# Delta rule in a hybrid layer: the correction of the chunk inverse in 16-bit pairs, its updates in place on the changed halves, the decay bias on ScalarE

## The chip, the core and the metric

The kernel runs on one core of one Trainium2 chip. The metric is the device time of one execution in microseconds; smaller is better. The engines are named as the profile names them: PE (TensorE, matmuls; PEld is its weight loads), DVE (VectorE), ACT (ScalarE), POOL (GpSimd) and SP (SyncE, which issues the DMAs).

## The reference

One layer of a hybrid encoder over 2048 prompt tokens and 64 tokens of a running stream, with 1024 features. RMSNorm and one input projection feed two groups: a gated delta rule with 4 heads of 128 and a multi-scale pooling group. Both go through one output projection, then a SwiGLU feed-forward and a final norm. Everything is float32. The change lies in the delta rule, which the reference computes by chunks in WY form (cut to what matters):

```python
G = jnp.cumsum(g, axis=-1)
gamma = jnp.exp(jnp.where(lower_incl, G[..., :, None] - G[..., None, :], -jnp.inf))
kb = k * beta[..., None]
Lm = jnp.where(lower_strict, jnp.einsum('bhncd,bhnsd->bhncs', kb, k) * gamma, 0.0)
T = lax.linalg.triangular_solve(eye + Lm, jnp.broadcast_to(eye, Lm.shape),
                                left_side=True, lower=True)
u = jnp.einsum('bhncs,bhnsv->bhncv', T, v * beta[..., None])
w = jnp.einsum('bhncs,bhnsk->bhnck', T, kb * jnp.exp(G)[..., None])
...
def step(S, xs):
    u_c, w_c, qk_c, qd_c, kt_c, dl_c = xs
    v_new = u_c - jnp.einsum('bhck,bhkv->bhcv', w_c, S)
    o_c = jnp.einsum('bhck,bhkv->bhcv', qd_c, S) + jnp.einsum('bhcs,bhsv->bhcv', qk_c, v_new)
    S = S * dl_c[..., None, None] + jnp.einsum('bhck,bhcv->bhkv', kt_c, v_new)
    return S, o_c
```

For every chunk of every head a unit triangular matrix is inverted; this inverse, and the decay matrix gamma, are what the change touches.

## The kernel before

The prompt is cut into four blocks of 512 tokens; the 64 tokens of the running stream ride with block 0. For each block the kernel projects (tiles `pp`, matmuls of 512 or 288 columns in a rounded 32-bit form, each product three matmuls of high and low parts), makes the decays (`rows`), and runs per head four chunks of 128 tokens. Between these run the pooling group and the output projection of the block before (tiles `pz`). After the last block follows the feed-forward, from 996 us on; it holds no work of the delta rule.

A head of a block is worked on by two kinds of chains. A *front* (`Front.all`, line 921) takes two chunks at once and needs no state: it makes the decay matrix, the products of k with k and q, and the inverse. There are 32 fronts of the prompt and one of the running stream. A *head* (`Head.prompt`, line 1071) then carries the state S through the chunks in order, with five small 32-bit matmuls per chunk (tiles `pk`, `po`).

In a front, every tile holds both chunks side by side, 128 partitions x 256 elements. These are its steps:

- **Decay.** `gb` gets the cumulated decay of each column by a matmul with `selp` (`rowmm`). ACT takes its exponential into EG. Then into the same bank go the mask `negm` (16-bit) and the negated decay of each row: two matmuls per front with `seln` as moving operand (`negmm`, line 908). ACT takes the exponential of all of it into `Gam`.
- **The matrix.** `gr` holds the products; U (tile `Gst`) is the strictly triangular matrix to be inverted (with 1 on the diagonal implied).
- **Levels.** The inverse T and its transpose V are built by doubling, seven levels for chunks of 128. In level l blocks of size 2^l are joined to blocks of twice that size. GpSimd masks U (`Um`), PE multiplies (`py`, 2 matmuls; ACT copies the result to `Yt`; `pt`, 4 matmuls), and DVE subtracts: `new` = TV - pt. These operands are 16-bit. TV holds T and V of both chunks, 512 elements, and is written anew in each level, in turns `TV0` and `TV1`, and in the last level in 32 bits, `TV32`.
- **Correction.** T from 16-bit arithmetic is corrected by two steps in 32 bits: F = I - T - U'T (GpSimd, `pf`, DVE), then T1 = V + F'V (`px0`, DVE) and X = V + F'T1 (`px1`, DVE). Each of the three products is one 32-bit matmul per chunk, so six in a front.

A bank of PSUM is set aside for each of three fronts that run at a time (`NLEV` = 3, banks b0 to b2); the tiles `gb`, `gr`, `py`, `pt`, `pf`, `px` of a front follow one another in its bank.

What sets the order: the kernel first records all operations, then a planner (`Machine.issue`) puts them on the engines' queues by its own reckoning of durations, dependences and ranks, and writes every engine's queue in that order. Therefore nearly all instructions have the line 278, and the views below go by tiles. On PE the planner prefers work of the fronts and heads and fills the gaps with dense matmuls. It places an instruction of PE 0.25 us behind the moment at which it reckons its operand ready (`MARGIN`). Each engine takes its queue strictly in that order. A 32-bit matmul stands as one instruction in the order and as two records in the trace.

Of the kernel before, what the change touches and what calls it, by code (L numbers as in the profile page):

```python
# [27 lines left out]
NH = 4  # L28
# [325 lines left out]
def hybrid_kernel(ctx, tc, a, o):  # L354
# [496 lines left out]
    nc.vector.tensor_copy(id16, ident)  # L851
    idbf = cp1.tile([P, P], BF16, tag="idbf", name="idbf")
# [7 lines left out]
    nc.vector.memset(Sp, 0.0)  # L860

# [6 lines left out]
    class Front:  # L868
# [39 lines left out]
        def negmm(self, ps):  # L908

            G = self.B.Ghl  # L910
            if self.h is None:
                for h in range(NH):
                    mm(ps[:, h * DEC : (h + 1) * DEC], G[:, SO : SO + P], seln[:, h, :].to_broadcast([P, DEC]),
                       start=False, stop=False)
            else:
                for c in range(2):
                    at = self.off + c * C
                    mm(ps[:, c * C : (c + 1) * C], G[:, at : at + C], seln[:, self.h, :].to_broadcast([P, C]),
                       start=False, stop=c == 1, skip_group_check=True)

        def all(self):
# [14 lines left out]
            for c in range(2):  # L936
# [17 lines left out]
            dd = gb if self.h is not None else self.ps(f"dd_{tag}")  # L954
            mm(dd[:, : 2 * C], idbf, bc(negm2 if self.h is None else negm, 2, C), start=dd is not gb, stop=False,
               skip_group_check=dd is gb)
            self.negmm(dd)
            if dd is not gb:
                self.rowmm(dd, False)
            Gam = self.QKG = gt([P, 2, C], F32, "Gam", NOUT)  # L960
            act(Gam, two(dd), AF.Exp)
# [17 lines left out]
            for l in range(nlev):  # L979
                Um = lev(F16, "Um", l, bufs=2)  # L980
                nc.gpsimd.tensor_tensor(out=Um, in0=U, in1=bc(lmask[:, l], 2, C), op=ALU.mult)
                new = TV32 if l == nlev - 1 else lev(F16, f"TV{l % 2}", l, [P, 2, 2, C])
# [3 lines left out]
                if l == 0:  # L986
                    idb = bc(id16, 2, C)
                    tt(new[:, 0], idb, two(py), ALU.subtract)
                    nc.gpsimd.tensor_tensor(out=new[:, 1], in0=idb, in1=Um, op=ALU.subtract)
                else:  # L990
# [796 lines left out]
```

## Time and profile before

| | us |
|---|---|
| Median of 3 runs | 2384.84 |
| Lowest and highest | 2381.84, 2387.46 |
| The profiled execution | 2383.12 |
| Its span, first to last instruction | 2380.5 |
| Mean granted clock of PE | 0.997 |

How to read the views used below. The page gives each engine's busy time. The view by stretches gives the same for parts of the span, in microseconds from its start. Rows of groups name engine, operation, tile written <- tiles read, shape and count, then busy time, mean duration in ns, and idle time before them with what ended it. Rows of a tile give minimum, median and maximum duration in ns. The waits of an engine give who waited <- for whom, the total, how often, and the longest. The timeline gives start, length of a run of equal instructions from first start to last end, and their count; consecutive matmuls overlap, since a matmul starts before the one ahead has drained. The chain of the work that ended last gives pieces with their start and length.

### The profile page before, as it was taken

The page shows a single profiled execution, that of the slowest core. Times are in us where ns is not written, and L with a number is a line of the kernel's source. Part 1 is how long each engine was busy: PE and PEld are TensorE (multiplying, and loading weights), DVE is VectorE, ACT ScalarE, POOL GpSimd, SP SyncE. Part 2 cuts the span into 40 slices and gives each one's busy share as a digit, 9 for nine tenths or more (in the row PEclk, how much of TensorE's full clock was granted, in tenths as well). Part 3 has the DMA queues.
Part 4 walks back from the last instruction along what each step waited for, and adds up shares of the span by engine and source line. Part 5 has one row for each costly group of instructions (what it writes and reads, how often), then busy time and mean ns, then how long its engine had stood idle before and what let it go on. Part 6 is the DMA issues. An engine that isn't in the chain of part 4 may idle for free.

```text
span 2380.5 us, 41651 instructions
## 1 busy us (share of the span) xinstructions
PE 2344.3 (98%) x14823; PEld 2184.7 (92%) x14823; DVE 1674.3 (70%) x2943; ACT 1215.7 (51%) x2738; POOL 967.2 (41%) x1130
## 2 busy tenths in 40 slices
PE   9999999999999999999999999999999999999998
PEld 8999798777887778899999999999999999999998
DVE  7999875785577686787776883767566657646466
ACT  6666654564456565574454654553334554425334
POOL 1656452554346662264332536353233464202211
PEclk9999999999999999999999999999999999999999
DMA  7643566445555565998876678887855697565763
GB/s 267 224 165 134 189 228 217 146 165 190 176 182 172 162 195 166 311 373 324 312 282 240 257 270 271 295 287 248 283 189 175 201 348 247 193 227 193 260 209 114
DMA packets 228384, 540.57 MB, mean 227 GB/s; under 512 B 28240, under 2 KB 86608, under 8 KB 228176
## 3 DMA queue, kind: packets, MB, share of 16 engines
q1 hardware_dynamic: 228176, 537.92, 66.2%
q8 instruction: 116, 1.90, 0.3%
q14 instruction: 92, 0.75, 0.1%
HBM read 389.41 MB, written 148.41 MB: 226 GB/s over the span
## 4 chain that ended last, share of the span: by engine, by line
PE 81%; DVE 9%; ACT 3%; DMA 3%; issue 2%; SPq 1%; POOL 1%; DVEq 0%; POOLq 0%; ACTq 0%
PE px L278 19%; PE pp L278 14%; PE pz L278 11%; PE py L278 9%; PE d L278 8%; PE dx L278 5%; PE dy L278 3%; PE pk_p L278 2%; PE pt_p L278 1%; PE dz L278 1%; PE gr_p L278 1%; PE px_p L278 1%; DVE Yqk L278 1%; PE py_p L278 1%; ACT E L278 1%
## 5 line engine op out<-in xcount | busy, mean ns | idle before, releaser
L278 PE MATMUL pp<-h,wsp 128*128 128x512 f32 (+1 forms) x2480 | 562.1, 366 | 2.0 <-DVE h L278 1.7
L278 PEld LDWEIGHTS pp<-h,wsp 128*128 128x128 f32 x2480 | 402.3, 190 | 49.8 <-DVE h L278 2.6
L278 POOL TENSOR_TENSOR Um_p<-Gst_p,lmask 128x256 f16<-128x256 f32 x224 | 178.2, 809 | 109.6 <-PE py_p L278 80.9
L278 PE MATMUL pz<-op,wsp 128*128 128x512 f32 (+1 forms) x960 | 216.8, 366 | 3.4 <-ACT op L278 2.9
L278 PE MATMUL d<-h3l,wsd 128*128 128x352 f32 x1248 | 201.3, 322 | 0.2 <-DVE h3l L278 0.2
L278 PEld LDWEIGHTS d<-h3l,wsd 128*128 128x128 f32 x1248 | 199.1, 188 | 1.2 <-DVE h3l L278 0.7
L278 PEld LDWEIGHTS pz<-op,wsp 128*128 128x128 f32 x960 | 155.9, 190 | 23.2 <-ACT op L278 3.4
L278 DVE TENSOR_TENSOR TV_p<-TV_p,pt_p 128x512 f16<-128x512 f16 (+1 forms) x192 | 128.5, 681 | 48.7 <-PE pt_p L278 43.4
L278 PE MATMUL px<-hA,ws 128*128 128x352 f32 x792 | 141.2, 322 | 0.6 <-DMA ws<-g 0.6
L278 PE MATMUL pz<-hB,ws 128*128 128x352 f32 x792 | 139.6, 322 | 0.6 <-DMA ws<-g 0.6
L278 PE MATMUL px<-hBT,ws 128*128 128x352 f32 x792 | 137.8, 322 | 2.1 <-DVE u L278 2.1
L278 PE MATMUL px<-hBT,wsS 128*128 128x352 f32 x792 | 137.7, 322 | 2.0 <-ACT g L278 1.9
L278 PE MATMUL py<-hB,wsS 128*128 128x352 f32 x792 | 139.2, 322 | 0.1
L278 PE MATMUL px<-hA,wsS 128*128 128x352 f32 x792 | 137.4, 322 | 0.9 <-ACT g L278 0.9
L278 PE MATMUL py<-hA,wsS 128*128 128x352 f32 x792 | 137.1, 322 | 0.0
L278 ACT ACTIVATE hr<-g 128x352 f32<-128x352 f32 x132 | 65.6, 497 | 133.4 <-DVE g L278 133.4
L278 PEld LDWEIGHTS px<-hBT,wsS 128*128 128x128 f32 x792 | 128.2, 188 | 2.8 <-ACT g L278 2.8
L278 PEld LDWEIGHTS px<-hBT,ws 128*128 128x128 f32 x792 | 128.0, 188 | 2.9 <-DVE u L278 2.7
L278 PEld LDWEIGHTS px<-hA,ws 128*128 128x128 f32 x792 | 128.9, 188 | 1.0 <-DMA ws<-g 0.9
L278 PEld LDWEIGHTS pz<-hB,ws 128*128 128x128 f32 x792 | 128.6, 188 | 0.8 <-ACT hB L278 0.8
L278 PEld LDWEIGHTS px<-hA,wsS 128*128 128x128 f32 x792 | 128.3, 188 | 1.2 <-ACT g L278 1.1
L278 PEld LDWEIGHTS py<-hB,wsS 128*128 128x128 f32 x792 | 128.6, 188 | 0.4 <-ACT u L278 0.4
(686 smaller groups left out, 5354.5 us busy)
## 6 DMA issues: line engine op xcount, KB each, us to landing
wsS<-gS SPq DMA_DIRECT2D x176, 512.0 KB, 4.7
ws<-g SPq DMA_DIRECT2D x132, 512.0 KB, 4.6
wsp<-wnd SPq DMA_DIRECT2D x126, 512.0 KB, 3.3
gS<-wsS SPq DMA_DIRECT2D x88, 512.0 KB, 5.6
g<-ws SPq DMA_DIRECT2D x66, 512.0 KB, 5.5
wnd<-wsp SPq DMA_DIRECT2D x42, 512.0 KB, 4.5
xd<-x2d SPq DMA_DIRECT2D x96, 176.0 KB, 4.0
wrd<-in_wd_dram SPq DMA_DIRECT2D x48, 256.0 KB, 4.7
```

The costliest lines, as they stand in the source:

```text
L278: getattr(getattr(self.nc, op.eng), name)(*args, **kw)
```

## The change

- **Correction.** T and V stay 16-bit in the last level too, and `TV32` is gone. U is split into a high and a low 16-bit half, scaled by 256 (`Uhl`, made by ACT and DVE behind level 2). `pf` is then four 16-bit matmuls. F is made on DVE in 32 bits from a 16-bit I - T (GpSimd) and `pf`, and split into halves `Fhl` (ACT, DVE). The first `px` takes the high half alone, two 16-bit matmuls; ACT scales it to 16 bits (`FV`, listed as Ytg). The second `px` stays in the same bank and adds three 16-bit matmuls per chunk: low half of F times V, T against a scaled identity `idfs` (which gives 256 V), high half of F times FV. ACT writes X from it. Both additions on DVE go.
- **Updates in place.** In level l only half of the columns of T and the other half of those of V change. DVE now subtracts on these alone, in one tile TV, through the view `fresh`: runs of 2^l elements with gaps of the same length, 256 elements in place of 512.
- **Decay.** The fronts of the prompt lose the two `seln` matmuls. ACT takes the exponential of each chunk with the negated decay as its bias per partition (`NG`, made once per block in `rows`), so Gam is two instructions of 128 elements. The running stream keeps the old way.
- EG moves from the first part of `TV32` to the tile tag `F`.

```diff
+    idfs = cp1.tile([P, P], F16, tag="idfs", name="idfs")
+    ts(idfs, ident, FS, None, ALU.mult)
...
+    def fresh(t, s):
+
+        (row, n), _ = t.ap
+        return bass.AP(t.tensor, t.offset, [[row, n], [2 * C + s, 2], [2 * s, 2 * C // (2 * s)], [1, s]])
...
-            TV32 = lev(F32, "TV32", "", [P, 2, 2, C])
...
-            EG = TV32[:, 0]
+            EG = lev(F32, "F", "e")
...
-            act(Gam, two(dd), AF.Exp)
+                mm(gb[:, : 2 * C], idbf, bc(negm, 2, C), start=False, stop=True, skip_group_check=True)
+                for c in range(2):
+                    act(Gam[:, c], two(gb)[:, c], AF.Exp, bias=self.B.NG[:, self.c0 + c, self.h : self.h + 1])
...
-                    tt(new, TV, pt.rearrange("p (t c n) -> p t c n", t=2, n=C), ALU.subtract)
-                TV = new
+                    new = fresh(TV.rearrange("p t c n -> p (t c n)"), 1 << l)
+                    tt(new, new, fresh(pt, 1 << l), ALU.subtract)
+                if l == 2:
+                    Uhl = lev(F16, "Uhl", "", [P, 2, 2, C])
+                    act(Uhl[:, 0], U, AF.Copy, scale=FS)
+                    stt(Uhl[:, 1], U, FS, Uhl[:, 0], ALU.mult, ALU.subtract)
                 yield LAT_TV
-            T, V = TV32[:, 0], TV32[:, 1]
-            F = lev(F32, "F")
-            nc.gpsimd.tensor_tensor(out=F, in0=bc(ident, 2, C), in1=T, op=ALU.subtract)
+            T, V = TV[:, 0], TV[:, 1]
+            F0 = lev(F16, "Um", "f", bufs=2)
+            nc.gpsimd.tensor_tensor(out=F0, in0=bc(id16, 2, C), in1=T, op=ALU.subtract)
             pf = self.ps(f"pf_{tag}")
             for c in range(2):
-                mm(pf[:, c * C : (c + 1) * C], U[:, c], T[:, c], start=True, stop=True)
-            tt(F, F, two(pf), ALU.subtract)
+                for i in range(2):
+                    mm(pf[:, c * C : (c + 1) * C], Uhl[:, i, c], T[:, c], start=i == 0, stop=i == 1)
+            F = lev(F32, "F")
+            stt(F, F0, FS, two(pf), ALU.mult, ALU.subtract)
+            Fhl = lev(F16, "Fhl", "", [P, 2, 2, C])
+            nc.scalar.copy(Fhl[:, 0], F)
+            tt(Fhl[:, 1], F, Fhl[:, 0], ALU.subtract)
             yield LAT_F
-            px = self.ps(f"px0_{tag}")
+            px = self.ps(f"px_{tag}")
             for c in range(2):
-                mm(px[:, c * C : (c + 1) * C], F[:, c], V[:, c], start=True, stop=True)
-            tt(T, V, two(px), ALU.add)
+                mm(px[:, c * C : (c + 1) * C], Fhl[:, 0, c], V[:, c], start=c == 0, stop=True, skip_group_check=c > 0)
+            FV = lev(F16, "Yt", "g")
+            act(FV, two(px), AF.Copy, scale=1.0 / FS)
             yield LAT_D
             yield self.before(NX, "used")
             X = self.X = gt([P, 2, C], F32, "X", NX)
-            px = self.ps(f"px1_{tag}")
             for c in range(2):
-                mm(px[:, c * C : (c + 1) * C], F[:, c], T[:, c], start=True, stop=True)
-            tt(X, V, two(px), ALU.add)
+                for i, (lhsT, rhs) in enumerate(((Fhl[:, 1, c], V[:, c]), (T[:, c], idfs), (Fhl[:, 0, c], FV[:, c]))):
+                    mm(px[:, c * C : (c + 1) * C], lhsT, rhs, start=False, stop=i == 2, skip_group_check=True)
+            act(X, two(px), AF.Copy, scale=1.0 / FS)
...
+        NG = B.NG = gp.tile([P, 4, NH], F32, tag="NG", name=f"NG{j}", bufs=2)
+        act(NG[:, :nch], pcs[:, :, :NH], AF.Copy, scale=-1.0)
...
+FS = 256.0
```

How the order changes, at three places. First PE, in the correction of the second front of head 1 in block 1; `pz` are dense matmuls of an output projection. Before:

```order
L278 MATMUL pf_p_1_1_1254<-TV_p_1_1_1141,Gst_p_1_1_1146 128x128 x2
L278 MATMUL pz_5_288_1170<-op_0_165,wsp_36_1070 128x288 x10
L278 MATMUL pz_5_288_1170<-op_0_164,wsp_36_1068 128x288
L278 MATMUL px_p_1_1_1258<-TV_p_1_1_1141,F_p_1_1_1253 128x128 x2
L278 MATMUL pz_5_288_1170<-op_0_164,wsp_36_1068 128x288 x11
L278 MATMUL px_p_1_1_1266<-TV_p_1_1_1141,F_p_1_1_1253 128x128 x2
```

The changed kernel at the same front, from the first `px` on:

```order
L278 LDWEIGHTS Fhl_p_1_1_1235
L278 MATMUL px_p_1_1_1238<-TV_p_1_1_1155,Fhl_p_1_1_1235 128x128
L278 LDWEIGHTS Fhl_p_1_1_1235
L278 MATMUL px_p_1_1_1238<-TV_p_1_1_1155,Fhl_p_1_1_1235 128x128
L278 MATMUL pz_6_0_1166<-op_0_167,wsp_37_1080 128x288 x9
L278 MATMUL pz_6_0_1166<-op_0_166,wsp_37_1078 128x288
L278 LDWEIGHTS Fhl_p_1_1_1235
L278 MATMUL px_p_1_1_1238<-TV_p_1_1_1155,Fhl_p_1_1_1235 128x128
L278 LDWEIGHTS TV_p_1_1_1155
L278 MATMUL px_p_1_1_1238<-idfs,TV_p_1_1_1155 128x128
L278 LDWEIGHTS Fhl_p_1_1_1235
L278 MATMUL px_p_1_1_1238<-Ytg_p_1_1_1239,Fhl_p_1_1_1235 128x128
```

Each product still stands between dense matmuls; the last one is six matmuls (three of them shown) where two stood, every one with a weight load of its own. Second PE, at the decay of the second front of head 2 in block 1, before:

```order
L278 MATMUL gb_p_2_1_1314<-Ghl_822,selp 128x256
L278 MATMUL rpn_20_1279<-lon_20_1281,onesr 128x512
L278 MATMUL pp_12_0_1276<-h_1_774,wsp_42_1222 128x512 x3
L278 MATMUL pp_13_0_1292<-h_1_773,wsp_43_1245 128x512 x3
L278 MATMUL gr_p_2_0_1323<-Yqk_2_1218 128x256
L278 LDWEIGHTS idbf
L278 MATMUL gb_p_2_1_1314<-negm,idbf 128x256
L278 MATMUL gr_p_2_0_1323<-Yqk_2_1218 128x256
L278 MATMUL gb_p_2_1_1314<-seln,Ghl_822 128x128 x2
```

and in the changed kernel:

```order
L278 MATMUL gb_p_2_1_1291<-Ghl_804,selp 128x256
L278 MATMUL pp_12_0_1253<-h_1_743,wsp_42_1198 128x512 x5
L278 LDWEIGHTS idbf
L278 MATMUL gb_p_2_0_1285<-negm,idbf 128x256
L278 LDWEIGHTS idbf
L278 MATMUL gb_p_2_1_1291<-negm,idbf 128x256
L278 MATMUL po_p_2__1455<-Qd_p_2_0_1288,Sp 128x128
```

The two `seln` matmuls are gone, and nothing of PE stands between the mask and ACT's exponential. Third DVE, at the end of the levels of the front of the first place, where `wsp` are splits of weights and `xc` evictions of an output projection. Before:

```order
L278 TENSOR_TENSOR TV_p_1_1_1141<-TV_p_1_1_1228,pt_p_1_1_1248 128x512
L278 TENSOR_TENSOR xc_0_1157<-pz_5_0_1158,xc_0_1157 128x288
L278 TENSOR_TENSOR F_p_1_1_1253<-F_p_1_1_1253,pf_p_1_1_1254 128x256
L278 TENSOR_TENSOR TV_p_1_1_1141<-TV_p_1_1_1141,px_p_1_1_1258 128x256
L278 TENSOR_TENSOR wsp_38_1126<-wrp_38_1125,wsp_38_1126 128x512
L278 TENSOR_TENSOR xc_288_1169<-pz_5_288_1170,xc_288_1169 128x288
L278 TENSOR_TENSOR X_p_1_1_1265<-TV_p_1_1_1141,px_p_1_1_1266 128x256
```

and in the changed kernel:

```order
L278 TENSOR_TENSOR TV_p_1_1_1155<-TV_p_1_1_1155,pt_p_1_1_1228 128x2x2x64
L278 TENSOR_TENSOR xc_0_1135<-pz_5_0_1136,xc_0_1135 128x288
L278 SCALAR_TENSOR_TENSOR F_p_1_1_1234<-Umf_p_1_1_1232,pf_p_1_1_1233 128x256
L278 TENSOR_TENSOR wsp_38_1106<-wrp_38_1105,wsp_38_1106 128x512
L278 TENSOR_TENSOR Fhl_p_1_1_1235<-F_p_1_1_1234,Fhl_p_1_1_1235 128x256
```

The update is half as long, and both additions of `px` have left DVE's queue; the low half of F has come.

More of the change, by code (lines that the diff above doesn't have):

```diff
@@ L910, in negmm @@
             G = self.B.Ghl
[L911 to L919, printed above, removed]
+            for h in range(NH):
+                mm(ps[:, h * DEC : (h + 1) * DEC], G[:, SO : SO + P], seln[:, h, :].to_broadcast([P, DEC]),
+                   start=False, stop=False)
         def all(self):
@@ L953, in all @@
             tt(Qd, self.Yqk[:, 0, self.off : self.off + 2 * C].rearrange("p (c n) -> p c n", n=C), EG, ALU.mult)
[L954 to L958, printed above, removed]
-                self.rowmm(dd, False)
-            Gam = self.QKG = gt([P, 2, C], F32, "Gam", NOUT)
-            act(Gam, two(dd), AF.Exp)
+            Gam = self.QKG = gt([P, 2, C], F32, "Gam", NOUT)
+            if self.h is None:
+                dd = self.ps(f"dd_{tag}")
+                mm(dd[:, : 2 * C], idbf, bc(negm2, 2, C), start=True, stop=False)
+                self.negmm(dd)
+                self.rowmm(dd, False)
+                act(Gam, two(dd), AF.Exp)
+            else:
+                mm(gb[:, : 2 * C], idbf, bc(negm, 2, C), start=False, stop=True, skip_group_check=True)
+                for c in range(2):
+                    act(Gam[:, c], two(gb)[:, c], AF.Exp, bias=self.B.NG[:, self.c0 + c, self.h : self.h + 1])
             U = lev(F32, "Gst")
```

9 lines of the change are left out of this document (5 added, 4 removed).

## The prediction

> **What bounds the kernel now.** I read the page first, then the busy time by stage, then TensorE's (PE's) waits, then the timeline of PE where the changed step runs. The page:
>
> ```profile
> span 2380.5 us, 41651 instructions
> ## 1 busy us (share of the span) xinstructions
> PE 2344.3 (98%) x14823; PEld 2184.7 (92%) x14823; DVE 1674.3 (70%) x2943; ACT 1215.7 (51%) x2738; POOL 967.2 (41%) x1130
> ```
>
> PE is busy 98% of the span. That share alone does not prove it (ends of matmuls are modelled), so I cut the span into the stage in which the fronts run, 60 to 950 us, and the feed-forward stage behind it.
>
> ```profile
> core 0: us, PE busy (x) PEld busy (x) DVE busy (x) ACT busy (x) POOL busy (x), PEclk, DMA share, GB/s
> ...
> 60.00:240.00 180.00, 177.97 (x1466) 165.96 (x1466) 169.81 (x346) 115.67 (x298) 109.72 (x158) 1.00 0.52 176
> 240.00:400.00 160.00, 157.09 (x1053) 138.23 (x1053) 110.38 (x201) 85.48 (x199) 59.20 (x78) 1.00 0.65 217
> 400.00:600.00 200.00, 199.65 (x1229) 159.05 (x1228) 142.55 (x254) 107.38 (x279) 100.39 (x140) 1.00 0.49 166
> 600.00:800.00 200.00, 196.54 (x1156) 158.28 (x1155) 135.11 (x236) 112.66 (x288) 100.41 (x141) 0.99 0.52 170
> 800.00:950.00 150.00, 145.76 (x877) 118.12 (x876) 117.38 (x203) 78.81 (x191) 77.64 (x97) 0.99 0.60 182
> ...
> 1000.00:2380.00 1380.00, 1361.66 (x8476) 1352.95 (x8474) 917.82 (x1529) 646.66 (x1326) 504.56 (x480) 1.00 0.73 253
> ```
>
> In the five pieces of the front stage PE is busy 177.97 + 157.09 + 199.65 + 196.54 + 145.76 = 877.0 of 890 us, at a granted clock of 0.99 to 1.00: 13 us idle in all. DVE is busy 675 us there (76%), ACT 500 (56%), and only in the first piece does another engine come near, DVE with 169.81 of 180 (94%). So what a microsecond of PE work is worth in this stage is nearly a microsecond. And PE hardly waits for the fronts' operands:
>
> ```profile
> PE pk_p L278 <- DVE Sp L278: 1.7, 1, 1.7
> PE pt_p L278 <- ACT Yt_p L278: 1.4, 2, 0.9
> ...
> PE ptv_p L278 <- DVE X_p L278: 0.7, 1, 0.7
> ...
> PE py_p L278 <- DVE TV_p L278: 0.7, 2, 0.5
> ...
> PE px_p L278 <- DVE TV_p L278: 0.4, 1, 0.4
> ```
>
> These five waits come to 4.9 us for 33 fronts. The order puts dense matmuls between the dependent ones of a front, and they hide its chain. Two things follow: shortening the chain on DVE or ACT can win at most a few microseconds, and taking matmul time off PE wins nearly all of it.
>
> **The price of a matmul.** Busy times of small groups hold the drain of each, so I price by starts, from one start to the next.
>
> ```profile
> L278 PE MATMUL pf_p<-TV_p,Gst_p x128: 270/275/328, 90.3 to 941.6; 128*128 128x128 f32 x128
> ...
> L278 PE MATMUL px_p<-TV_p,F_p x256: 270/275/377, 92.8 to 946.2; 128*128 128x128 f32 x128
> ```
>
> ```profile
> 386.03 15.43 PE pp L278 x68
> ```
>
> ```profile
> 401.30 0.60 PE L278 MATMUL ptk_p<-consts,Yqk 128*128 128x128 f32 x4
> ```
>
> ```profile
> 422.27 0.40 PE L278 MATMUL py_p<-TV_p,Um_p 128*128 128x128 f16 x4
> 422.47 1.87 PE L278 MATMUL pp<-h,wsp 128*128 128x512 f32 x7
> 424.19 0.28 PE L278 MATMUL pt_p<-Yt_p,TV_p 128*128 128x128 f16 x2
> 424.31 0.28 PE L278 MATMUL pt_p<-TV_p,Yt_p 128*128 128x128 f16 x2
> 424.42 0.28 PE L278 MATMUL pt_p<-Yt_p,TV_p 128*128 128x128 f16 x2
> 424.53 0.28 PE L278 MATMUL pt_p<-TV_p,Yt_p 128*128 128x128 f16 x2
> 424.62 2.33 PE L278 MATMUL pp<-h,wsp 128*128 128x512 f32 x9
> ...
> 439.71 0.41 PE L278 MATMUL gb_p<-seln,Ghl 128*128 128x128 f32 x2
> 439.96 0.45 PE L278 MATMUL pp<-h,wsp 128*128 128x512 f32 x1
> ```
>
> ```profile
> 490.03 1.64 PE L278 MATMUL pp<-h,wsp 128*128 128x512 f32 x6
> 491.51 0.39 PE L278 MATMUL pk_p<-vn_p,ktl_p 128*128 128x128 f32 x2
> 491.73 0.39 PE L278 MATMUL po_p__1571<-Gam_p,vn_p 128*128 128x128 f32 x2
> 491.88 1.63 PE L278 MATMUL pp<-h,wsp 128*128 128x512 f32 x6
> ```
>
> A 32-bit matmul of 128 columns stands as two records (64 matmuls pf_p, 128 records). Four records last 0.60 us where one lasts 0.275: (0.60 - 0.275)/3 = 0.108 each; two last 0.39: 0.115. I take 0.111 a record, 0.222 a matmul. 16-bit ones start 0.34 us apart over six (424.19 to 424.53), 0.057 each, and eight with the change to the next kind take 0.43, 0.054 each: I take 0.056.
>
> A change of kind costs too. Undisturbed dense matmuls start every 15.43/68 = 0.227 us. Between two 16-bit groups seven take 424.19 - 422.47 = 1.72, which is 0.13 more than 7 x 0.227; the 16-bit groups themselves run 0.02 short of n x 0.056, so a 16-bit excursion costs 0.11 beside its matmuls. Around 32-bit groups six take 491.51 - 490.03 = 1.48, 0.12 more, but four records then take 0.37 in place of 0.44: 0.05 net, or less. A 16-bit excursion is some 0.07 us dearer than a 32-bit one.
>
> **The change part by part.**
>
> The correction on PE. A front (32 of the prompt, one of the sample) loses six 32-bit matmuls (two pf, four px): 198 x 0.222 = 44.0 us off. It gains four 16-bit ones for pf, two for the first px, six for the second: 396 x 0.056 = 22.2 us on. Bounds of the latter: 0.054, and above by the load of a 16-bit weight if none were hidden behind the matmul before it:
>
> ```profile
> L278 PEld LDWEIGHTS <-Yt_p 128*128 128x128 f16 x384 | 29.6, 98 | 0.0
> ```
>
> 29.6/384 = 0.077 us of loading each, so 30.5 us on. The 16-bit steps py and pt have just this pattern (a new weight for every matmul), so I stay at 0.056. [...]
>
> The negated decay. The 64 matmuls of gb_p from seln go: at 0.111 they are 7.1 us (the two rows at 439.71 take 0.25 with the change of kind, so up to 8). In their place ACT adds the bias.
>
> Changes of kind, counted in the order of both kernels: dense to 32-bit falls from 207 to 150 places, dense to 16-bit rises from 247 to 302; the way back likewise (232 to 164, 222 to 288). Some 60 excursions turn from 32-bit to 16-bit: 60 x 0.07 = 4 us on. Bounds 0 and 8.
>
> DVE, ACT and GpSimd, with rows of these shapes:
>
> ```profile
> L278 DVE TENSOR_TENSOR TV_p<-TV_p,pt_p x192: 669/680/691, 67.3 to 940.0; 128x512 f16<-128x512 f16 x160, 128x512 f32<-128x512 f16 x32
> ...
> L278 DVE TENSOR_TENSOR TV_p<-id,py_p x32: 403/409/423, 63.5 to 915.4; 128x256 f16<-128x256 f16 x32
> ```
>
> ```profile
> L278 DVE TENSOR_TENSOR Qd_p<-Yqk,TV_p 128x256 f32<-128x256 f32 x32 | 15.3, 480 | 3.0 <-ACT TV_p L278 2.5
> L278 DVE TENSOR_TENSOR X_p<-TV_p,px_p 128x256 f32<-128x256 f32 x32 | 13.3, 416 | 9.9 <-PE px_p L278 9.9
> ```
>
> ```profile
> L278 ACT CAST Yt_p<-py_p 128x256 f16<-128x256 f32 x192 | 68.4, 370 | 113.3 <-PE py_p L278 112.7
> ...
> L278 ACT ACTIVATE vn_p<-pk_p,kn_p 128x128 f32<-128x128 f32 x64 | 23.6, 368 | 45.8 <-PE pk_p L278 45.7
> ...
> L278 ACT ACTIVATE Gam_p<-gb_p 128x256 f32<-128x256 f32 x32 | 12.2, 385 | 1.6 <-PE gb_p L278 1.4
> ```
>
> The six updates of T and V go from 512 to 256 elements, 0.68 to 0.41 us: 192 x 0.27 = 52 us off DVE. The two additions of px go to ACT: 64 x 0.416 = 27 off. Two low halves (Uhl, Fhl) come at about 0.48: 31 on. DVE loses some 48 us of 675. ACT gains per front two high halves (Uhl, Fhl), Ytg and X at about 0.37 to 0.41, and Gam becomes two instructions with a bias, 2 x 0.368 for 0.385: about 1.9 us a front, 61 us on 500, to 63% of the stage. GpSimd's subtraction stays one of 128x256. None of this is on PE's path while PE has dense work to put between; I cost it at nothing. Two instructions in ACT's queue now wait for px where DVE waited (9.9 us for X in the row above); behind them stand casts of weights, evictions and vn. If the cover fails, those 20 us of waiting over both additions are the price.
>
> In the chain of a front each level gets 0.27 us shorter, and the correction gets one more hand-over (F to its high half on ACT, about 0.4). The chain gets shorter by about 1.2 us, and PE's waits for it (4.9 us) are late next, from both sides a few microseconds.
>
> The feed-forward stage (1380 us above) is untouched, and the last 7991 rows of PE's order are the same in both kernels.
>
> The sum: -44.0 + 22.2 - 7.1 + 4 = -24.9 us. The profiled execution took 2383.1 us (its span of 2380.5 and 2.6 around it), 1.7 under the median of the three runs, 2384.84. I forecast the median: 2384.8 - 24.9 = 2360 us.
>
> **Rivals.**
>
> Weight loads not hidden (0.10): every added 16-bit matmul costs 0.077 us as its load does, and the changes of kind cost 8 us: -44.0 + 30.5 - 7.1 + 8 = -12.6, 2372 us. For it: PEld's busy share in the front stage is already high (165.96 of 180 in the first piece). Against it: the py and pt rows.
>
> Time handed to others (0.06): the freed PE time becomes idle time, since DVE at 94% in the first piece, or the arrival of weights, sets the pace. In the first piece alone (8 of 33 fronts) that would take back 6 us, 2366. For no measurable change it must take back 20 of 25; the DMA share of 0.49 to 0.65 and DVE's lighter load speak against it.
>
> PE meets the fronts too early, and the kernel gets slower (0.07). PE takes its queue in order, so an operand that comes later than the order reckons stalls the dense matmuls behind it. The halved update now reads and writes runs of 2, 4, 8 up to 64 elements with gaps, which no row of this trace shows. If each of the six updates and of the three hand-overs of the correction, 297 in all, came w late at PE, the gain would be gone at w = 25/297 = 0.085 us; at w = 0.15 it is -25 + 45 = +20, 2405 us. The order allows 0.25 us of slack for PE over its reckoned durations, so it decides where an update lasts more than about 0.41 + 0.25 + 0.085 = 0.75 us, twice the dense row. Against it: the strided form handles half the elements, and even at one and a half times the time for each it ends before the 0.68 of today. [...]
>
> The change not doing what it says: the matmuls of pf and px are 16-bit in the order, so only the price is open.
>
> **How the numbers follow.** Forecast 0.74, the rivals 0.10, 0.06 and 0.07, and 0.03 for a larger gain (waits of PE that go as well). Low end: 16-bit at 0.054 (21.4), 32-bit at 0.115 (45.5), the negated decay at 8, changes of kind at 0, and 3 of the 4.9 us of waits gone: -35, 2350 us. High end: just over the first rival, 2373 us. A measurement of this kernel tells about 0.2% (4.8 us) from no change. Faster by more: 0.74 + 0.10 + 0.03 = 0.87. Within 0.2%: 0.06, slower 0.07.
>
> **What would show it.** In the profile after: no rows gb_p from seln; pf_p and px_p as 16-bit with 0.055 to 0.06 us between starts; PE's busy time in the front stage lower by about 25 us and the stage shorter by as much; the updates of T and V at 0.41 us for each stride; DVE near 1626 us, ACT near 1277. I am wrong if PE's waits for TV_p, Fhl_p or Ytg_p exceed 10 us, if the small updates last over 0.6 us, or if PE is idle over 30 us in the front stage.

## The result and the profile after

The changed kernel takes 2355.74 us, median of 4 runs (2352.81 to 2357.52); the kernel before, run beside it, 2385.63 us. The ratio is 0.9881 with a 95% interval of 0.9869 to 0.9893: 28 us faster. The forecast was 2360, with a range of 2350 to 2373. Its total held. How it was split over the three parts of the change did not, and most of what follows is on that.

The page of the changed kernel, its first lines:

```profile
span 2354.1 us, 41684 instructions
## 1 busy us (share of the span) xinstructions
PE 2318.9 (99%) x14759; PEld 2151.3 (91%) x14759; DVE 1642.4 (70%) x2944; ACT 1263.8 (54%) x2906; POOL 978.3 (42%) x1130
```

PE is busy 25.4 us less (2344.3 before), and the span is 26.4 us shorter. DVE loses 32 us, ACT gains 48. The view by stretches of the changed kernel, with the columns as before:

```profile
core 0: us, PE busy (x) PEld busy (x) DVE busy (x) ACT busy (x) POOL busy (x), PEclk, DMA share, GB/s
60.00:240.00 180.00, 178.04 (x1488) 163.25 (x1486) 163.15 (x353) 131.46 (x348) 117.87 (x162) 1.00 0.55 186
240.00:400.00 160.00, 158.16 (x1063) 139.13 (x1064) 108.58 (x212) 98.51 (x249) 61.18 (x84) 1.00 0.64 217
...
1000.00:2354.00 1354.00, 1332.87 (x8282) 1323.63 (x8280) 899.84 (x1497) 624.94 (x1284) 486.70 (x468) 1.00 0.72 249
```

PE is as full as before; DVE fell from 169.81 to 163.15 in the first piece, ACT rose from 115.67 to 131.46. The tiles that the change touches, with minimum, median and maximum duration in ns:

```profile
L278 PE MATMUL pf_p<-TV_p,Uhl_p x128: 216/219/233, 87.0 to 911.2; 128*128 128x128 f16 x128
L278 PE MATMUL px_p<-TV_p,Fhl_p x128: 219/219/233, 89.8 to 914.6; 128*128 128x128 f16 x128
L278 DVE TENSOR_TENSOR TV_p<-TV_p,pt_p x192: 398/415/423, 65.9 to 909.7; 128x256 f16<-128x256 f16 x192
L278 DVE TENSOR_TENSOR Fhl_p<-F_p,Fhl_p x32: 409/424/1503, 89.8 to 912.4; 128x256 f16<-128x256 f32 x32
L278 DVE SCALAR_TENSOR_TENSOR Uhl_p<-Gst_p,Uhl_p x32: 411/606/932, 60.3 to 883.3; 128x256 f16<-128x256 f32 x32
```

The updates last 0.415 us at the median, and none of the 192 more than 0.423, whatever the length of their runs. The second px of one front, in the timeline of PE (start, length, count):

```profile
309.54 0.22 PE L278 MATMUL px_p<-TV_p,Fhl_p 128*128 128x128 f16 x1
309.60 0.22 PE L278 MATMUL px_p<-idfs,TV_p 128*128 128x128 f16 x1
309.65 0.22 PE L278 MATMUL px_p<-Ytg_p,Fhl_p 128*128 128x128 f16 x1
309.71 0.22 PE L278 MATMUL px_p<-TV_p,Fhl_p 128*128 128x128 f16 x1
309.76 0.22 PE L278 MATMUL px_p<-idfs,TV_p 128*128 128x128 f16 x1
309.82 0.22 PE L278 MATMUL px_p<-Ytg_p,Fhl_p 128*128 128x128 f16 x1
309.88 0.39 PE L278 MATMUL pf_p<-TV_p,Uhl_p 128*128 128x128 f16 x4
```

From the first start to the seventh it is 309.88 - 309.54 = 0.34 us: 0.057 apart, each with a new weight. And PE's waits for the fronts and heads:

```profile
PE py_p L278 <- DVE TV_p L278: 2.4, 3, 1.7
...
PE pt_p L278 <- ACT Yt_p L278: 0.6, 2, 0.4
...
PE pk_p L278 <- DVE Sp L278: 0.3, 1, 0.3
PE pf_p L278 <- DVE TV_p L278: 0.3, 1, 0.3
```

These four come to 3.6 us, where the five before came to 4.9. The order still covers the chains, as far as this view tells.

**An account by starts.** To see where the time went, I took all matmul records of the front stage, from the first matmul to the first one of the feed-forward, and split every distance from one start to the next. The base is what such a record takes undisturbed (0.056 us for 16-bit, 0.111 for 32-bit, 0.227 and 0.126 for dense of 512 and 288 columns, the low end of their distances, whose medians are 0.231 and 0.133 in both traces; the few with other shapes at their own, most of them in the third row). An excess up to 0.13 us counts as a change of kind, a larger one as a stall, so the split between these two hangs on that bound. This is worked out from the traces; no view prints it. Microseconds, each kernel's profiled execution:

| | before | changed | difference | forecast |
|---|---|---|---|---|
| 32-bit, base | 187.0 | 143.3 | -43.7 | -44.0 |
| 16-bit, base | 73.5 | 95.7 | +22.2 | +22.2 |
| dense with the seln matmuls, base | 681.9 | 676.4 | -5.5 | -7.1 |
| changes of kind | 26.5 | 27.1 | +0.6 | +4 |
| stalls | 26.6 | 22.1 | -4.5 | 0 |
| front stage | 995.5 | 964.6 | -30.9 | -24.9 |

The first two differences agree with the forecast by their making: they are counts of matmuls times the prices that the forecast took. What the trace confirms is the price of the 16-bit ones, in the px rows above. In the third row the 64 `seln` matmuls are 7.1 us and the other shapes +1.6.

The feed-forward stage was 4.4 us longer in this pair of profiles (1375.3 and 1379.8 from first to last matmul). Its code is the same, and all fourteen traces of this study lie between 1374 and 1380, so I take that as spread.

The table already shows one thing that the prediction had not seen: the kernel before has 26.6 us of stalls by starts, where the views of waits showed 4.9 for the fronts. They hold, besides waits, what PE loses while it is granted half the clock (6.8 us of the front stage in this trace, 3.4 in that of the changed kernel, where dense matmuls of 512 columns start 0.427 us apart, against 0.231 at the median of the stage); e4 below comes back to that.

### The profile page after: what moved, and what is told of

Read it like the earlier page. It is cut to its first block, busy times and chain, and to the rows that moved or that the text cites. A ratio compares the mean times of both kernels' runs of the same rounds, so it can differ in the third digit from the quotient of the medians.

```text
span 2354.1 us, 41684 instructions
## 1 busy us (share of the span) xinstructions
PE 2318.9 (99%) x14759; PEld 2151.3 (91%) x14759; DVE 1642.4 (70%) x2944; ACT 1263.8 (54%) x2906; POOL 978.3 (42%) x1130
## 4 chain that ended last, share of the span: by engine, by line
PE 83%; DVE 8%; DMA 4%; issue 2%; ACT 2%; POOL 1%; SPq 1%; DVEq 0%; POOLq 0%; ACTq 0%
PE px L278 19%; PE pp L278 15%; PE pz L278 12%; PE py L278 9%; PE d L278 8%; PE dx L278 6%; PE dy L278 3%; PE pk_p L278 2%; PE pt_p L278 2%; PE dz L278 1%; PE gr_p L278 1%; PE py_p L278 1%; DVE Yqk L278 1%; DVE y L278 1%; DMA xh<-hpd 1%
## 5 line engine op out<-in xcount | busy, mean ns | idle before, releaser
L278 POOL TENSOR_TENSOR Um_p<-Gst_p,lmask 128x256 f16<-128x256 f32 x224 | 184.7, 838 | 89.4 <-PE py_p L278 59.8
L278 PEld LDWEIGHTS py<-hA,wsS 128*128 128x128 f32 x792 | 128.6, 188 | 0.0
```

Of the source, the lines that this page charges most:

```text
L278: getattr(getattr(self.nc, op.eng), name)(*args, **kw)
```

## The experiments

The theory after the result was that of the prediction: PE's own matmul time makes the gain, the correction (-44.0 + 22.2 + 4 = -17.8 by the sum, put at -16 before its run) and the decay (-7), and the halved updates bring nothing, since PE seldom waits for them. The rival: part of the gain comes through DVE, whose queue reaches PE in places that the waits do not show. e5 adds matmuls and e6, e7 and e9 add instructions on DVE whose results nobody reads; the times of the changed kernel below are the 2355.74 above, and each kernel's ratio is to the kernel before on its chip. That took 2385.63 beside the changed kernel, 2385.42 beside e1 to e4, 2383.29 beside e5 to e8 and 2384.32 beside e9 to e12, so a difference of medians across these groups is known to some 2 us, beside the spread of each.

**Each part alone.** Three kernels with one part of the change each, all else as in the kernel before.

e1, the correction alone. The updates stay whole, in two 16-bit tiles by turns, and the decay is as before. Against the changed kernel:

```diff
-                    new = fresh(TV.rearrange("p t c n -> p (t c n)"), 1 << l)
-                    tt(new, new, fresh(pt, 1 << l), ALU.subtract)
+                    new = lev(F16, f"TV{l % 2}", l, [P, 2, 2, C])
+                    tt(new, TV, pt.rearrange("p (t c n) -> p t c n", t=2, n=C), ALU.subtract)
+                    TV = new
...
+            act(Gam, two(dd), AF.Exp)
...
```

> Only the correction in 16-bit pairs; updates full (512 elements, 16-bit, two tiles in turn), decay by the two negated matmuls as before. Theory (PE's matmul time sets the stage): -44.0 for 198 32-bit matmuls, +22.2 for 396 16-bit ones, and 6 for the changes of kind (its order has 325 entries into 16-bit groups and 155 into 32-bit ones, before 247 and 207): -16 us, about 2370. Rival (the gain came from DVE's shorter updates and the shorter chain): within 5 us of the kernel before, about 2385, or slower, since the chain has a hand-over more.

Measured: 2375.95 us (2373.49 to 2378.87), ratio 0.9961 [0.9949, 0.9974], 9.5 us gained in place of 16.

e2, the updates alone: in place and halved on levels 1 to 5; the last level still writes all of `TV32`.

```diff
+                    if l == nlev - 1:
+                        tt(TV32, TV, pt.rearrange("p (t c n) -> p t c n", t=2, n=C), ALU.subtract)
+                    else:
+                        new = fresh(TV.rearrange("p t c n -> p (t c n)"), 1 << l)
+                        tt(new, new, fresh(pt, 1 << l), ALU.subtract)
```

> Only the updates in place on the changed halves in levels 1 to 5 (the last level writes the 32-bit tile in full, as before); correction in 32 bits, decay as before. 160 of 192 updates go from 0.68 to 0.41 us on DVE, 43 us in all. Theory (PE's matmul time): no change, within 4 us of the kernel before, 2382 to 2388, since PE's matmuls are the same. Rival (DVE at 94% in the first piece and the chain set the pace): faster by 8 us or more.

Measured: 2377.93 us (2374.25 to 2378.36), ratio 0.9966 [0.9953, 0.9978]: 7.5 us gained, where the theory had 0.

e3, the decay alone:

```diff
+                mm(gb[:, : 2 * C], idbf, bc(negm, 2, C), start=False, stop=True, skip_group_check=True)
+                for c in range(2):
+                    act(Gam[:, c], two(gb)[:, c], AF.Exp, bias=self.B.NG[:, self.c0 + c, self.h : self.h + 1])
...
```

> Only the decay bias on ACT; the two negated matmuls a front go, the rest as before. Theory: 64 x 0.111 = 7 us faster, 2378 to 2380, with PE's excursions as many as before (454). Rival (ACT's second instruction of 0.37 us lengthens the chain at its start, and PE waits): no gain or slower.

Measured: 2373.36 us (2371.81 to 2375.88), ratio 0.9952 [0.994, 0.9965]: 12 us in place of 7.

All three forecasts missed, by 5 to 8 us, while the sum of the three results, -9.5 - 7.5 - 12.0 = -29.0, is near the gain of the whole (28.4 by the ratio, 29.9 by the medians). The account by starts says what happened in e1: base -43.8 and +22.2 as in the whole change, changes of kind +5.0 (forecast +4), but stalls +4.3, so with 0.3 in the dense ones -12.0 for the stage. The added stalls are in the first piece: 10.9 us between 60 and 240 us, where the kernel before has 4.2. The view by stretches of e1, its first piece:

```profile
60.00:240.00 180.00, 173.12 (x1432) 157.82 (x1430) 169.52 (x332) 124.92 (x325) 106.66 (x155) 0.99 0.52 172
```

PE's busy time falls from 177.97 to 173.12 there: PE has less to do per front, DVE (169.52) has as much as before, and PE gives time back as stalls. One such place in the timeline of PE of e1; the brackets are idle time and who ended it:

```profile
159.95 0.28 PE L278 MATMUL pt_p<-Yt_p,TV_p 128*128 128x128 f16 x2
160.06 0.28 PE L278 MATMUL pt_p<-TV_p,Yt_p 128*128 128x128 f16 x2
160.35 0.49 PE L278 MATMUL pk_p<-vn_p,ktl_p 128*128 128x128 f32 x2
160.68 0.39 PE L278 MATMUL po_p__514<-Gam_p,vn_p 128*128 128x128 f32 x2
161.84 0.27 PE L278 MATMUL py_p<-TV_p,Um_p 128*128 128x128 f16 x2 [0.78 <-DVE TV_p L278]
162.44 0.27 PE L278 MATMUL py_p<-TV_p,Um_p 128*128 128x128 f16 x2 [0.33 <-DVE TV_p L278]
162.70 0.49 PE L278 MATMUL pk_p<-Sp,Yqk 128*128 128x128 f32 x2
```

and of DVE at the same time:

```profile
159.00 0.35 DVE L278 SCALAR_TENSOR_TENSOR rhs_p<-pk_p,EC,vtk_p 128x128 f32<-128x128 f32 x1
159.26 1.93 DVE L278 TENSOR_TENSOR wsp<-wrp,wsp 128x512 fp32r<-128x512 f32 x2
161.12 1.27 DVE L278 TENSOR_TENSOR TV_p<-TV_p,pt_p 128x512 f16<-128x512 f16 x2
```

The last matmuls of pt, of both fronts (those of the other start at 159.73, not shown), end at 160.34. Yet the first update starts only at 161.12: it stands behind two subtractions for weights (1.93 us) on DVE. PE, with no dense matmul in its order there, has a distance of 1.16 us from the start at 160.68 to that at 161.84, where two 32-bit records take 0.22. And the second update, of another front, ends 0.6 us behind the first, so the second py stands too. A short update shortens both waits. That DVE's queue is what PE meets here is the rival's mechanism.

**The changed kernel with whole updates (e4).** The same lines as in the first part of e1's diff, and nothing else (cut):

```diff
-                    tt(new, new, fresh(pt, 1 << l), ALU.subtract)
+                    new = lev(F16, f"TV{l % 2}", l, [P, 2, 2, C])
+                    tt(new, TV, pt.rearrange("p (t c n) -> p t c n", t=2, n=C), ALU.subtract)
...
```

> The changed kernel with the updates undone: DVE subtracts all 512 elements in each level again (16-bit, two tiles in turn). Theory (PE's matmul time): within 4 us of the changed kernel, 2355 to 2361, though DVE is 51 us busier. Rival (the 5 us by which the change gained more than the sum came from DVE's relief): 2361 to 2366.

Measured: 2370.8 us (2368.95 to 2373.32), ratio 0.9941 [0.9929, 0.9954]: 15 us lost, more than either forecast had. Undoing the halved updates thus takes back half of the whole gain, once the other two parts are in. By starts the stage is 16.4 us longer: stalls are 34.5 us against 22.1, and changes of kind 29.0 against 27.1; the base differs by 2.1. The two pieces with the largest difference, in the view by stretches of e4 (the changed kernel has PE at 178.04 and 146.90, DVE at 163.15 and 117.92 there):

```profile
60.00:240.00 180.00, 174.37 (x1439) 159.74 (x1438) 169.35 (x340) 127.31 (x338) 108.64 (x157) 0.98 0.55 175
...
800.00:950.00 150.00, 143.68 (x838) 111.19 (x837) 120.69 (x202) 88.74 (x218) 74.91 (x85) 0.98 0.65 194
```

PE's views of waits hardly tell: they name `py_p <- TV_p` and `pf_p <- TV_p`, and give them 6.5 us together.

```profile
PE py_p L278 <- DVE TV_p L278: 4.0, 5, 1.6
...
PE pf_p L278 <- DVE TV_p L278: 2.5, 2, 1.6
```

In the changed kernel the same two, shown above, stand at 2.4 and 0.3: a difference of 3.8 us where the time differs by 15.

Part of the 15 us comes by the granted clock, which in every trace of this study is 1 or 0.5. In e4 PE has half the clock for 20.4 us of the front stage (from 60 us on), in four stretches, against 3.4 us in the changed kernel. One of them, in the view by stretches, and the stall at its start:

```profile
218.10:224.90 6.80, 5.54 (x31) 4.57 (x31) 5.78 (x14) 2.23 (x6) 3.17 (x7) 0.50 0.00 0
```

```profile
217.22 0.27 PE L278 MATMUL pt_s<-TV_s,Yt_s 128*128 128x128 f16 x2
219.11 0.58 PE L278 MATMUL pf_p<-TV_p,Uhl_p 128*128 128x128 f16 x4 [1.61 <-DVE TV_p L278]
```

In that stretch dense matmuls of 288 columns start 0.24 us apart, behind it 0.133. Half of 20.4 - 3.4 us is 8.5 us, an upper estimate of what the clock takes of the 16.4; the account lists it partly as stalls, partly as changes of kind. The mean clock of the five timed executions, 0.993 to 0.995 against 0.996 to 0.997, fits. Each of the four stretches follows 1.7 us or more of stalls within 3.4 us, so the whole updates probably stand behind it too, but what DVE's time costs PE without the clock was not measured apart.

**The price of a 16-bit matmul (e5).** Twelve more per front behind the second px, 396 in all, into an unused half of its bank:

```diff
+            for i in range(6):
+                for c in range(2):
+                    mm(px[:, (c + 2) * C : (c + 3) * C], (T, V)[i % 2][:, c], Fhl[:, 0, c], start=False, stop=i == 5,
+                       skip_group_check=True)
```

> The changed kernel with 12 more 16-bit matmuls a front (396 in all), behind the second px in the unused half of its bank; nothing reads their result. Theory (0.056 us each where the weight loads are hidden): 22.2 us, less 2 for the order's fewer changes of kind, so 20 slower than the changed kernel, 2376. [...]

Measured: 2372.92 us (2370.36 to 2376.91), ratio 0.9956 [0.9944, 0.9969]: 17 us for 396, 0.043 each. A group of them in the timeline of PE of e5:

```profile
312.77 0.83 PE L278 MATMUL px_p<-Fhl_p,TV_p 128*128 128x128 f16 x12
```

(0.83 - 0.22)/11 = 0.055 us from start to start. The added base is some 22 us by that, and the stalls are 2.3 us fewer; that more work on PE covers DVE a little better would fit, but was not shown. Had every load stood in the open at the prediction's 0.077 us, it would be 30 us; this run has 17.

**What time on DVE is worth (e6, e7, e9).** Two small products (128x64, 0.225 us each at the median) are put on DVE's queue at each update, unknown to the planner, so that every order stays as it is. In e6 they stand ahead of the update, in e7 behind it, where they delay only what comes next on DVE. e9 is e6 with the planner told of 0.5 us more per update.

```diff
+            for _ in range(LATE if op.extra is not None else 0):
+                self.nc.vector.tensor_tensor(out=op.extra[0], in0=op.extra[1], in1=op.extra[1], op=ALU.mult)
...
+                    machine.ops[-1].extra = late, ones[:, :64]
...
+LATE = 2
```

e9 adds:

```diff
+                    machine.ops[-1].occ += 0.500
+                    machine.ops[-1].lat += 0.500
```

> The changed kernel with two small extra instructions on DVE (128x64, result unused, some 0.4 to 0.5 us together) right ahead of each of the 192 updates of T and V; the planner does not reckon with them, so the order of all else is that of the changed kernel. DVE's work returns to more than that of the full updates, and every level ends 0.4 to 0.5 us later than reckoned, 0.25 of it covered by the margin. If the length of the chain is what the updates bought: 15 to 38 us slower, 2371 to 2394. If PE's waits are as small as the view of waits says (the theory so far): within 5 us of the changed kernel.

> The same two extra instructions on DVE right behind each update: DVE is as busy as in the run with them ahead, but the update itself ends on time. If the length of the chain is what counts: within 5 us of the changed kernel, 2352 to 2361. If DVE's occupancy is what counts (94% busy in the first piece): as slow as the run with them ahead, 2365 or more.

> As the run with the two extra instructions ahead of each update (0.45 us more on DVE each, 57 us slower than the changed kernel), but the planner reckons 0.5 us more for each update and lays the order out for it. Theory now (PE stalls because operands come later than its order reckons): most of the loss goes, as with the full updates, which the planner knew (51 us more of DVE, 15 us slower); at that rate 88 us of DVE cost 25 us, 2381. Rival (DVE's occupancy itself sets the pace): as slow as without the planner's knowledge, 2405 or more.

Measured: e6 2412.53 us (2412.16 to 2415.45), ratio 1.0126 [1.011, 1.0141]; e7 2405.55 (2402.88 to 2406.98), 1.0092 [1.0078, 1.0105]; e9 2419.67 (2418.06 to 2421.57), 1.0148 [1.0133, 1.0164]. e6 is above both of its forecasts; e7 and e9 came out near what their rivals had. The added work in e6, by the tile with minimum, median and maximum, and as a group with busy time and mean:

```profile
L279 DVE TENSOR_TENSOR late<-ones x394: 205/225/1316, 66.9 to 969.9; 128x64 f32<-128x64 f32 x197
```

```profile
L279 DVE TENSOR_TENSOR late<-ones 128x64 f32<-128x64 f32 x394 | 146.6, 372 | 6.8
```

The mean is far above the median: the 204 products of e6 during which GpSimd does nothing last 0.228 us at most, the 190 beside an instruction of GpSimd 0.534 on average. So the added time is not 394 x 0.225 = 89 us. DVE's busy time on the pages of e6, e7 and e9 (the changed kernel has 1642.4):

```profile
PE 2335.1 (97%) x14759; PEld 2156.8 (89%) x14759; DVE 1757.1 (73%) x3338; ACT 1270.3 (53%) x2906; POOL 974.3 (40%) x1130
```

```profile
PE 2337.8 (97%) x14759; PEld 2159.1 (90%) x14759; DVE 1747.1 (73%) x3338; ACT 1267.8 (53%) x2906; POOL 966.6 (40%) x1130
```

```profile
PE 2346.2 (97%) x14759; PEld 2163.7 (90%) x14759; DVE 1756.2 (73%) x3338; ACT 1266.5 (52%) x2906; POOL 967.5 (40%) x1130
```

115, 105 and 114 us more on DVE cost 57, 50 and 64 us. So it matters little whether the time stands ahead of the update or behind it: what was put behind one update stands ahead of something else that PE needs, in e7 the next update, `rhs_p` and `Sp`. PE's waits of e6, one line, and of e7:

```profile
PE py_p L280 <- DVE TV_p L280: 32.8, 59, 2.0
```

```profile
PE py_p L278 <- DVE TV_p L278: 16.1, 23, 2.0
PE pk_p L278 <- DVE rhs_p L278: 3.7, 6, 1.3
```

In these runs PE pays for DVE's time wherever it is put, more than for the length of one chain. e9 bears on another theory: that the loss comes from the planner's not knowing. Told of it, the planner made an order that is no faster, 2419.67 where that theory had 2381, so the theory fell. How much worse the order itself is stays open, since e9 also has half the clock for 40.9 us of its front stage, e6 for 3.4 and e7 for 20.4. The first piece in the views of e6, e7 and e9, one each:

```profile
60.00:240.00 180.00, 165.37 (x1333) 148.41 (x1332) 171.31 (x415) 123.05 (x322) 101.27 (x146) 0.99 0.50 165
```

```profile
60.00:240.00 180.00, 167.48 (x1344) 151.28 (x1343) 169.81 (x415) 121.61 (x320) 100.04 (x147) 0.97 0.50 167
```

```profile
60.00:240.00 180.00, 161.17 (x1253) 143.91 (x1253) 165.15 (x386) 118.95 (x310) 93.74 (x138) 0.94 0.48 160
```

DVE doesn't get beyond 171 of 180 us (95%), near where it stood before the change (169.81), and PE falls from 178.04 to 161 to 167. This suggests that DVE stood near its limit in this piece in the kernel before already.

But the cost is not confined to that piece. PE's order is the same in e6, e7 and the changed kernel, so the time of the same matmuls can be compared. Those that take the changed kernel from 60 to 240 us take 23.2 us longer in e6 and 21.9 in e7, where DVE is busy 28.1 and 25.5 us more. Those from 240 to 950 us take 35.9 and 32.2 us longer, for 88.3 and 81.3 us of DVE. A microsecond of DVE thus cost some 0.8 in the first piece, where DVE is busy 91% of the time in the changed kernel, and still 0.4 behind it, where it is busy 62 to 79%. This too is worked out from the traces; no view prints it.

**Fewer changes of kind (e8).** The planner may hold small matmuls back while it is in dense ones; a longer hold makes 372 excursions of 452.

```diff
-HOLD = 0.4, 3.0
+HOLD = 0.8, 3.0
```

> The changed kernel with one number of the planner changed: it keeps PE on dense matmuls until a matmul of a front has been ready for 0.8 us instead of 0.4, so that more of them go together. The order has 372 excursions from dense matmuls in place of 452 (225 into 16-bit, 147 into 32-bit groups, before 302 and 150). Theory (a 16-bit excursion costs 0.11 us beside its matmuls): 77 x 0.11 = 8 us faster, 2348, less what the later chain costs. Rival (excursions are cheap, the chain counts): no gain or slower, 2356 to 2365.

Measured: 2363.97 us (2359.96 to 2367.09), ratio 0.9918 [0.9904, 0.9931]: 8 us slower in place of 8 faster. By starts the front stage is 6.6 us longer (971.2 for 964.6). Stalls rise from 22.1 to 31.3, all of it behind 800 us (16.8 for 6.9), so the rest of the stage is 2.6 us shorter: fewer changes of kind may pay that much, where the forecast had 8. Behind 800 us lies also a stretch of 10.2 us at half the clock (3.4 in the changed kernel), which by the same estimate costs up to 3.4 us more; that the last chains have no dense work left there to cover a delay was not shown. In the view by stretches of e8 PE falls from 146.90 to 139.73 there:

```profile
800.00:950.00 150.00, 139.73 (x803) 108.68 (x803) 113.46 (x203) 88.26 (x219) 64.12 (x73) 0.97 0.63 191
```

So this run doesn't give the price of an excursion by itself: that stays open. The clock in this line is 0.97 over 150 us.

**Versions that follow from this (e10, e11, e12).** e10 drops the 66 matmuls with `idfs`, which add V to px on PE; DVE adds V as it writes X, in place of ACT. e11 moves the low half of F from DVE to GpSimd. e12 has both.

```diff
-                for i, (lhsT, rhs) in enumerate(((Fhl[:, 1, c], V[:, c]), (T[:, c], idfs), (Fhl[:, 0, c], FV[:, c]))):
+                for i, (lhsT, rhs) in enumerate(((Fhl[:, 1, c], V[:, c]), (Fhl[:, 0, c], FV[:, c]))):
...
-            act(X, two(px), AF.Copy, scale=1.0 / FS)
+            stt(X, two(px), 1.0 / FS, V, ALU.mult, ALU.add)
```

```diff
-            tt(Fhl[:, 1], F, Fhl[:, 0], ALU.subtract)
+            nc.gpsimd.tensor_tensor(out=Fhl[:, 1], in0=F, in1=Fhl[:, 0], op=ALU.subtract)
```

> The changed kernel without the matmuls of T against the scaled identity: 66 16-bit matmuls fewer on PE, 3.7 us; DVE adds V when it scales px into X, 32 x 0.41 = 13 us more of DVE, ACT as much less. If only PE's matmul time counted: 2352. If DVE's time costs PE 15/51 = 0.29 of itself, as with the full updates: -3.7 + 3.9, no change, 2356.

> The changed kernel with the low half of F subtracted on GpSimd instead of DVE: 33 x 0.42 = 14 us off DVE, about 0.8 us a front on GpSimd, which is not waited for until the second px. If DVE's time costs PE 0.29 of itself: 4 us faster, 2352. If PE's matmul time alone counts: no change, 2356.

> Both together: no identity matmuls, and the low half of F on GpSimd. PE loses 3.7 us of matmuls and DVE's work stays as in the changed kernel (13 on, 14 off). Theory now (matmul time plus DVE's share): 2352, faster than both kernels. Rival (GpSimd's later low half makes PE wait at the second px): 2356 or more.

Measured: e10 2346.78 us (2343.39 to 2347.73), ratio 0.984 [0.9825, 0.9855]; e11 2351.95 (2350.43 to 2356.51), 0.9869 [0.9853, 0.9885]; e12 2347.1 (2345.08 to 2347.87), 0.9843 [0.9828, 0.9857]. e10 is the fastest kernel of this study, 37.5 us under the kernel before and 9 under the changed one. It gains more than either forecast. Of the 8.1 us between the two profiled executions 2.1 lie in the feed-forward stage, whose code is the same. By starts the front stage is 6.0 us shorter than the changed kernel's: 3.7 for the matmuls, as counted, and 3.5 of stalls, with 1.2 the other way in the rest. DVE carries 32 x 0.412 = 13 us more for it:

```profile
L278 DVE SCALAR_TENSOR_TENSOR X_p<-px_p,TV_p x32: 406/412/427, 94.6 to 906.8; 128x256 f32<-128x256 f32 x32
```

At e6's rate (57 us for 115) this should have cost some 6.5 us, and no such cost can be seen. Yet DVE's busy time on its page is 1636.0 us, 6.4 less than the changed kernel's, since rows of tiles that the edit doesn't touch got shorter; so this run is no test of that rate. ACT has one instruction fewer that stands for px; that this is why was not shown. e11's gain over the changed kernel is 4 us, as forecast from DVE's time, but the two intervals overlap. Together (e12) they bring 9 us, more than the 4 that were forecast, and no more than e10 alone.

## Why the prediction was right, and where its steps failed

- **What bounds the kernel.** That PE sets the end held: its busy time fell by 25.4 us, the span by 26.4. But "PE hardly waits for the fronts' operands", 4.9 us, is the step that failed. (The list also left out a wait of a front, gb_p for ACT, 1.2 us.) The waits count idle time, and a record of a 128-column matmul lasts 219 ns where its successor may start 56 ns behind it; a delay shorter than what is left of that record shows as no idle time, and a longer one shows too short. By starts there were 26.6 us of stalls in all, up to 3.4 of them through the clock. The rows px_p above overlap (0.22 us long, 0.057 apart), and this overlap is what hides a stall.
- **The correction on PE.** Its prices held where they could be seen: 0.057 us from start to start in the px rows and 0.055 in e5 for the forecast's 0.056, and in e1 the changes of kind came to +5.0 for +4. But alone it was worth 9.5 us in place of 17.8, since the lighter PE ran into DVE in the first piece.
- **The decay.** -12 measured for -7.1. In the account of e3 the row that holds the seln matmuls is 5.8 us shorter, changes of kind 1.7 and stalls 2.1, less 1.2 in the 32-bit ones: 8.3 for the stage of the profiled execution, which is at the near end of the interval of the timed ones (8.3 to 14.3 us). Where the rest of the 12 comes from stays open.
- **DVE, ACT and GpSimd "at nothing".** Wrong for DVE. Its updates were worth 7.5 us alone and 15 beside the other two parts, up to half of these 15 through the clock. The duration was as forecast (0.415 for 0.41).
- **DVE and ACT busy.** 1642.4 for 1626. The two low halves add up to 39 us (0.679 us on average for Uhl, 0.550 for Fhl) where the prediction had 0.48 each and 31 us; that is 8 of these 16 us. The rest lies in rows of tiles that the change doesn't touch. ACT 1263.8 for 1277.
- **The rivals.** Weight loads not hidden: refuted by e5, 17 us for 396 matmuls where loads in the open would have cost 30. Time handed to others: its mechanism is real. In e1 stalls in the first piece take back 6.7 us, just the size that the rival had; in the whole change the halved updates pay for it. PE meeting the fronts too early: two products more at each update cost 50 to 64 us in e6, e7 and e9, so a late DVE does cost PE dearly; the strided updates simply did not last longer: the row TV_p of the changed kernel has 398/415/423 ns, the dense row of 256 elements in the kernel before 403/409/423.
- **The sum** came out within 4.3 us because two errors met: the correction alone brings 8 less than its terms, the updates and the decay 12 more. That they nearly cancelled was luck.

## What to carry to other kernels

An engine at 94% in one piece of the program can be a second bound there, even if the first engine seems to wait for it 5 us in all: with PE's work alone taken off (e1), PE gave 6.7 us of it back as stalls in that piece. Judge waits of PE by the distances between starts, not by idle time, and look at the granted clock in the same places. Price each part of a change with the other parts in as well as alone. When PE work is taken away, look for time to take off the engine that feeds it in the same edit. And price added work by the mean of its rows, or by the engine's busy time, not by the median.

## What the runs showed of the hardware that was not expected

- An update in place with runs of 2 to 64 16-bit elements and gaps of the same length took what the dense one took: 0.415 us at the median and 0.423 at most in the 192 of the changed kernel, against 0.409 and 0.423 for the 32 dense ones of 256 elements in the kernel before, both with one operand in PSUM.
- Half the clock was seen behind short stalls. In the fourteen traces the granted clock is 1 or 0.5, and a stretch at 0.5 inside the front stage lasts 3.4 us or two to four times that. The front stages from 60 us on have 3.4 us of it in the changed kernel, 6.8 in the kernel before, 20.4 in e4 and e7, 40.9 in e9 and none in e10. In the 3.4 us ahead of each such stretch there are 1.3 to 3.2 us of stalls by starts. Not every stall was followed by one: e6 has more stalls than e7 (some 80 us by starts against some 70) and only 3.4 us of half the clock in its trace, and in the first piece a mean clock of 0.99 with PE busy 165 of 180 us, where e7 has 0.97 with 167.
- Some DVE instructions whose two operands both lie in SBUF lasted several times as long beside an instruction of GpSimd. The added products of e6 last up to 1.316 us beside one and 0.228 at most without. The low half of F (both operands in SBUF) lasts 0.426 us at most in the 15 fronts where GpSimd does nothing beside it, and up to 1.503 in the 17 others. The low half of U, 0.606 at the median, stands beside work of GpSimd in all 32 fronts. The updates of TV, with one operand in PSUM, last 0.423 at most in all 192, the 127 beside GpSimd included. No run took GpSimd's work away, so this is read from the traces alone.
